# A hybrid encoder layer on one Trainium2 core: buffers of their own for some raw weight blocks and for G, low parts of the weights last, squares tied to later casts

## The chip, the cores and the metric

The kernel runs on 1 core of one Trainium2 chip. The metric is the device time in microseconds (us) of one execution of the whole program; lower is better. It is written in Bass with the Tile framework: tile pools hand out buffers, a scheduler orders the instructions of most engines, and semaphores carry the dependences. The engines in play are the TensorE (PE: matmuls, with its weight loads, PEld), the VectorE (DVE), the ScalarE (ACT), GpSimd (POOL) and the SyncE (SP), whose queue starts nearly all DMAs.

## The reference

One layer with sandwich norms around both sub-layers. Batch 1, S = 512 positions, D = 2048, FF = 4096 (twice that in the up projection), all float32.

```python
h = rms_norm(x, norm_gains[l, 0])
(sb_q, ..., sc_x) = jnp.split(h @ w_in[l], 11, axis=-1)      # 2048 x 5632
# four head groups: stick-breaking and differential attention, RG-LRU, short convolution
mixed = jnp.concatenate([y_sb, y_df, y_lru, y_sc], axis=-1) @ w_out[l]   # 2048 x 2048
x = x + rms_norm(mixed, norm_gains[l, 1])
h = rms_norm(x, norm_gains[l, 2])
u = causal_dwconv(h @ ffn_w_up[l], ffn_conv_w[l])            # 2048 x 8192, three taps
g, up = jnp.split(u, 2, axis=-1)
x = x + rms_norm((gelu(g) * up) @ ffn_w_down[l], norm_gains[l, 3])   # 4096 x 2048
```

## The kernel before

**Split numbers.** Activations lie transposed, as tiles of 128 channels by 512 positions. Each float32 operand is split into a high part, rounded to the matmul's type (float32r), and a low part, the rest. A product is three matmuls: high by high, high by low, low by high (`matmul3`, L120 to L125). Weights come from memory as raw blocks of 512 KB, 128 x 1024 numbers (`chunk`, L88 to L101, buffers `w_raw`); the ScalarE casts the high part (`w_hi`, L99), the VectorE subtracts to get the low part (`w_lo`, L100). Each of these three names has three buffers in the pool `wp`.

**Stages**, with their place in the profiled span:
- 0 to about 640 us: the in projection in `group`s, with the four head groups' work beside it.
- To about 775 us: the out projection (`out_group`); its last two groups of columns are done for each half of the positions apart (`HALVES`, 256 wide). `SumSq` (from L770) gathers the sum of squares for a norm: the ScalarE squares, GpSimd adds (L785), and a matmul with ones (L795) adds over the partitions, with the last `direct` squares given to that matmul apart. `residual` (L807) scales the result, has GpSimd's DMA accumulate it into x (L818), squares the sum on the ScalarE (L822), adds the squares (L824), stores the new x, called x1 (L826), and scales it by the gains (L829). `norm2` makes the normed h with its high and low parts.
- 775 to about 873 us: `up_plain`, units 0 to 3 of the up projection in ordinary groups. `low_parts` (L883) makes the last low parts of h out of the tiles gh and gl, which are then free.
- 873 to 1531 us: 28 calls of `up_unit` (L977), units 4 to 31. Each multiplies a 2 x 2 arrangement of weight blocks a11, a12, a21, a22 with h in seven products instead of eight (Strassen's scheme), of 24 matmuls 128 x 256 each. The operands of the products are a11, a12, s2, s1, s3, s4, a22 in this order, with s3 = a11 + a21, s1 = a21 + a22, s2 = a11 + s1, s4 = a12 + s2. s1 is made by a DMA of GpSimd that accumulates a22 from memory into a21's tile (L1017); the other sums are adds on the VectorE (L995). `operand` (L987 to L990) splits each into `w_hi` (ScalarE) and `w_lo` (VectorE). The products' results go from their accumulators to the tiles `ub` by copies on the ScalarE (L1026, L1036, L1041, L1053) and adds on the VectorE (L1032, L1045, L1049); then come the convolution (L928, L930), the gelu (L933), the gated product (L938), called g, and its store to memory (`g_d`, L939).
- 1540 to about 1896 us: g is loaded back (L1082) and split into high and low parts (L160, L161), and the down projection runs in groups over it. The last norm and x1 (loaded again, L1107) make the output (`finish`, L1108 to L1111).

**What sets the order.** PE issues in the order in which the program is written (`manual_schedule`). `tick()` counts blocks of matmuls, and `at(block, fn)` places work beside a given block. The other engines are ordered by the scheduler with priorities; work under `high_priority(offset=AHEAD)` goes ahead. Each engine, and SP's queue too, works its list in order: an instruction that waits holds all behind it.

**Buffers around the change.** In a unit, a11, a21 and a12 are in the three buffers of `w_raw`; s3 and a22 (loaded a second time, L1037) are in the halves of gh and gl (`spare`, two of each, which alternate from unit to unit). In the down projection the tiles f that hold loaded g and x1 come from the pool t3f with 5 buffers, opened where the pools of the up projection have been closed.

Of the kernel before, what the change touches and what calls it, by code (L numbers as in the profile page):

```python
# [16 lines left out]
P = 128  # L17
# [31 lines left out]
def trunk(ctx: ExitStack, tc: tile.TileContext, xT, params, consts, wgate, w_in, w_out, w_up0, w_up, w_dn, out):  # L49
# [30 lines left out]
    def gain(i, k):  # L80
        return pc("g", i * KT + k)
# [38 lines left out]
    def matmul3(ps, sh, sl, mh, ml, first, last, more=False):  # L120

        kw = {"skip_group_check": True} if more else {}
        T.matmul(ps, lhsT=sh, rhs=mh, start=first, stop=False, **kw)  # L123
        T.matmul(ps, lhsT=sh, rhs=ml, start=False, stop=False, **kw)  # L124
        T.matmul(ps, lhsT=sl, rhs=mh, start=False, stop=last, **kw)  # L125

    def group(chunks, hi, lo, order, evac, pool_tile=mm_tile, ts=ALL, before=None, tokens_out=False):
# [5 lines left out]
        for c in range(n):  # L133
# [3 lines left out]
            wh, wl = chunks[c]() if callable(chunks[c]) else chunk(chunks[c], 2 if fine else 1)  # L137
            for u, kk in ([(u, kk) for kk in range(2) for u in range(4)] if fine else
# [619 lines left out]
    with ExitStack() as ph:  # L758
        big = ph.enter_context(tc.tile_pool(name="bigf", bufs=4))
        ffp = ph.enter_context(tc.tile_pool(name="ffp", bufs=2))  # L760
        up_ph = ph.enter_context(ExitStack())
        ph2 = up_ph.enter_context(tc.tile_pool(name="ph2", bufs=1))
        t2p = up_ph.enter_context(tc.tile_pool(name="t2f", bufs=8))
# [45 lines left out]
        def residual(hf):  # L809
# [167 lines left out]
        def up_unit(unit):  # L977
            src = w_up[unit - 4]

            def raw(a, b):  # L980
                with tc.high_priority(offset=AHEAD):
                    t = wp.tile([P, 2, S], F32, name="w_raw")
                    nc.sync.dma_start(out=t, in_=src[a, b])
                return by4(t)
# [12 lines left out]
            def product(ps, ops, name, first):  # L997
                hi, lo = ops
                th, tl = tops[name]
                for k in range(8):  # L1000
# [227 lines left out]
```

## Time and profile before

| what | us |
|---|---|
| median of 3 runs (lowest, highest) | 1920.5 (1918.5, 1921.66) |
| the profiled execution | 1920.45 |
| its span, first to last instruction | 1918.7 |
| PE busy | 1803.0 |
| PE waiting for a low part in the units (L990) | 54.0 |
| mean granted clock of PE | 0.981 |

The prediction shows the page's lines. In them PE, PEld, DVE, ACT, POOL and SP are the engines; SPq and POOLq are the queues of DMAs of an engine. A row of the waits gives who waited for whom: us in total, times, and the longest. A row of the timeline gives the start, the duration, engine, line, operation, the tile written and those read, and in brackets how long the engine was idle before it and what ended this. A row of the windows gives a stretch, its length, the busy time of each engine with its number of instructions, the granted clock, the DMA share and GB/s. A row of DMA issues gives the number, the size, and the median time from issue to landing.

### The profile page before, as it was taken

How to read it: one execution, taken by the hardware profiler on the slowest of the kernel's cores; microseconds unless marked ns; L12 is line 12 of the kernel's file. 1: busy time of each engine (PE TensorE's matmuls, PEld its weight loads, DVE VectorE, ACT ScalarE, POOL GpSimd, SP SyncE). 2: the span in 40 equal slices, each digit the busy share in tenths (PEclk: the TensorE clock that was granted, in tenths of full speed). 3: DMA queues.
4: the chain of work that ended last, by engine and by line, in shares of the span. 5: the costliest groups of instructions: out<-in, count | busy, mean ns of one | idle time of the engine just before them, and what ended most of it. 6: DMA issues, size and time to landing. Idle time of an engine off the chain costs nothing. (4 is left out here: it accounts for less than half of the span.)

```text
span 1918.7 us, 27629 instructions
## 1 busy us (share of the span) xinstructions
PE 1803.0 (94%) x11176; PEld 1621.4 (85%) x11176; DVE 1145.5 (60%) x1574; ACT 869.5 (45%) x1301; POOL 110.9 (6%) x163
## 2 busy tenths in 40 slices
PE   8999999999999998898998998899999889999995
PEld 6778788888888898897988888888988878888895
DVE  7883675756574247598766666666666762222364
ACT  6442676743343347574444444444444552221342
POOL 0000111100000112100000000000000000010101
PEclk9999999999999999898999999999999999999998
DMA  7234222333325358755444444444444483333465
GB/s 242 86 102 132 76 72 83 110 116 90 98 88 197 102 181 235 216 178 153 123 122 123 133 121 122 121 123 126 128 126 128 119 285 99 99 97 94 125 200 182
DMA packets 84073, 256.91 MB, mean 134 GB/s; under 512 B 9029, under 2 KB 13381, under 8 KB 83945
## 3 DMA queue, kind: packets, MB, share of 16 engines
q1 hardware_dynamic: 78184, 235.23, 39.5%
q0 software_dynamic: 5184, 18.88, 5.1%
q8 instruction: 87, 1.43, 0.3%
q10 hardware_dynamic: 576, 1.05, 0.1%
q14 instruction: 42, 0.34, 0.1%
HBM read 230.99 MB, written 21.24 MB: 131 GB/s over the span
## 5 line engine op out<-in xcount | busy, mean ns | idle before, releaser
L124 PE MATMUL mm<-al,w_hi 128*128 128x256 f32 (+1 forms) x2048 | 674.4, 329 | 0.0
L125 PE MATMUL mm<-ah,w_lo 128*128 128x256 f32 (+1 forms) x1824 | 615.8, 338 | 54.9 <-DVE w_lo L990 53.4
L123 PE MATMUL mm<-ah,w_hi 128*128 128x256 f32 (+1 forms) x1824 | 618.2, 339 | 8.1 <-ACT w_hi L99 6.9
L100 DVE TENSOR_TENSOR w_lo<-w_raw,w_hi 128x1024 fp32r<-128x1024 f32 (+1 forms) x249 | 306.2, 1230 | 406.0 <-ACT w_hi L99 405.3
L99 ACT CAST w_hi<-w_raw 128x1024 fp32r<-128x1024 f32 (+1 forms) x249 | 260.6, 1047 | 449.5 <-PE mm L124 285.9
L125 PEld LDWEIGHTS mm<-ah,w_lo 128*128 128x128 f32 x1824 | 351.5, 193 | 98.3 <-DVE w_lo L990 62.3
L124 PEld LDWEIGHTS mm<-al,w_hi 128*128 128x128 f32 x2048 | 395.7, 193 | 31.5 <-issue 1.0
L123 PEld LDWEIGHTS mm<-ah,w_hi 128*128 128x128 f32 x1824 | 351.7, 193 | 41.1 <-ACT w_hi L99 7.3
L989 ACT CAST w_hi<-w_raw 128x1024 fp32r<-128x1024 f32 x140 | 145.9, 1042 | 222.8 <-PE mm L124 128.3
L990 DVE TENSOR_TENSOR w_lo<-w_raw,w_hi 128x1024 fp32r<-128x1024 f32 x140 | 170.6, 1219 | 2.6 <-ACT w_hi L989 2.6
L123 PE MATMUL mm<-big,w_hi 128*128 128x256 f32 (+1 forms) x544 | 161.6, 297 | 8.5 <-ACT big L160 8.5
L125 PE MATMUL mm<-big,w_lo 128*128 128x256 f32 (+1 forms) x544 | 163.1, 300 | 0.3
L124 PE MATMUL mm<-big,w_hi 128*128 128x256 f32 (+1 forms) x544 | 161.2, 296 | 0.0
L995 DVE TENSOR_TENSOR w_raw<-w_raw 128x1024 f32<-128x1024 f32 x56 | 68.4, 1222 | 138.6 <-DMA w_raw<-in_w_up_dram 138.6
L123 PE MATMUL pa<-ah,w_hi 128*128 128x256 f32 (+1 forms) x384 | 117.2, 305 | 3.3 <-ACT w_hi L99 3.3
L125 PE MATMUL pa<-ah,w_lo 128*128 128x256 f32 (+1 forms) x384 | 117.2, 305 | 2.2 <-DVE w_lo L100 2.2
L124 PE MATMUL pa<-al,w_hi 128*128 128x256 f32 (+1 forms) x384 | 116.6, 304 | 0.0
L123 PEld LDWEIGHTS mm<-big,w_hi 128*128 128x128 f32 x544 | 104.4, 192 | 11.4 <-ACT big L160 8.8
L125 PEld LDWEIGHTS mm<-big,w_lo 128*128 128x128 f32 x544 | 104.2, 192 | 6.7 <-DVE w_lo L990 4.2
L124 PEld LDWEIGHTS mm<-big,w_hi 128*128 128x128 f32 x544 | 104.4, 192 | 3.0 <-DVE big L161 0.4
L123 PE MATMUL mm<-gh,w_hi 128*128 128x256 f32 (+1 forms) x320 | 100.3, 314 | 1.9 <-ACT ub L1026 1.9
L125 PE MATMUL mm<-gh,w_lo 128*128 128x256 f32 (+1 forms) x320 | 98.2, 307 | 0.6 <-DVE w_lo L990 0.6
(266 smaller groups left out, 2659.4 us busy)
## 6 DMA issues: line engine op xcount, KB each, us to landing
w_raw<-in_w_up_dram SPq DMA_DIRECT2D x116, 512.0 KB, 4.2
w_raw<-in_w_in_dram SPq DMA_DIRECT2D x87, 512.0 KB, 3.6
w_raw<-in_w_dn_dram SPq DMA_DIRECT2D x80, 512.0 KB, 3.7
w_raw<-in_w_out_dram SPq DMA_DIRECT2D x48, 512.0 KB, 3.6
gl<-in_w_up_dram SPq DMA_DIRECT2D x28, 512.0 KB, 7.0
w_raw<-in_w_up_dram POOLq DMA_DIRECT2D x28, 512.0 KB, 8.0
g_d<-f SPq DMA_DIRECT2D x32, 256.0 KB, 4.3
f<-g_d SPq DMA_DIRECT2D x32, 256.0 KB, 4.1
```

Source lines behind the costliest of these rows:

```text
L99: w_split.append(A.copy(out=hi[:, sl], in_=raw[:, sl]))
L100: V.tensor_tensor(out=lo[:, sl], in0=raw[:, sl], in1=hi[:, sl].bitcast(F32), op=ALU.subtract)
L123: T.matmul(ps, lhsT=sh, rhs=mh, start=first, stop=False, **kw)
L124: T.matmul(ps, lhsT=sh, rhs=ml, start=False, stop=False, **kw)
L125: T.matmul(ps, lhsT=sl, rhs=mh, start=False, stop=last, **kw)
L989: w_split.append(A.copy(out=by4(hi), in_=v))
L990: V.tensor_tensor(out=by4(lo), in0=v, in1=by4(hi).bitcast(F32), op=ALU.subtract)
L995: V.tensor_tensor(out=out, in0=a, in1=b, op=ALU.add)
```

## The change

Three things change in the kernel, and some buffers move with them.

1. In `group`, each chunk but the last (and but a first one that comes in two pieces) now issues its sixteen matmuls with the weights' high part first and the eight with the low part after them; so does `product` in a unit.
2. a11 and a21 of a unit are loaded into the halves of gh and gl; s3, a12 and a22 go to the three buffers of `w_raw`. The tiles for loaded g, and half of those for x1, get a pool of their own (`ystage`, 3 buffers), open from the start of the phase; t2f has 6 buffers instead of 8, t3f 3 instead of 5. The last norm's `SumSq` have 3 square tiles, and the second one hands one square less to the matmul.
3. In `residual`, the squares of x1 and the scaling are issued block by block, each tied behind the most recent weight cast, and `norm2` comes 36 blocks later in both halves instead of 38 and 46.

```diff
     def group(chunks, hi, lo, order, evac, pool_tile=mm_tile, ts=ALL, before=None, tokens_out=False):
...
+            if not fine and c < n - 1:
+                for low in range(2):
+                    for u in range(4):
+                        us = slice(u * P, (u + 1) * P)
+                        for kk in range(2):
+                            k = order[2 * c + kk]
+                            if tokens_out:
+                                pairs = [(lo[k][:, us], wh[:, kk]), (hi[k][:, us], wh[:, kk])]
+                                pairs = [(hi[k][:, us], wl[:, kk])] if low else pairs
+                            else:
+                                pairs = [(wh[:, kk, us], hi[k][:, ts]), (wh[:, kk, us], lo[k][:, ts])]
+                                pairs = [(wl[:, kk, us], hi[k][:, ts])] if low else pairs
+                            for i, (a, b) in enumerate(pairs):
+                                T.matmul(pss[u], lhsT=a, rhs=b, start=c == 0 and kk == 0 and not low and i == 0,
+                                         stop=False)
+                        if u % 2 == 1:
+                            tick()
+                continue
...
+        ystage = ph.enter_context(tc.tile_pool(name="ystage", bufs=3))
...
-        t2p = up_ph.enter_context(tc.tile_pool(name="t2f", bufs=8))
+        t2p = up_ph.enter_context(tc.tile_pool(name="t2f", bufs=6))
...
                 G.dma_start(out=xs[q][:, hf], in_=mg[q][:, hf], accum_op=ALU.add)
-            for k in range(0, KT, 2):
-                x1 = xs[k // 4][:, hf, k % 4:k % 4 + 2]
-                sq = acc if k == 0 else ph2.tile([P, 2, S // 2], F32, name="q2", bufs=2)
-                A.activation(out=sq, in_=x1, func=AF.Square)
-                if k > 0:
-                    V.tensor_tensor(out=acc, in0=acc, in1=sq, op=ALU.add)
-                if k % 4 == 2:
-                    nc.sync.dma_start(out=x1_d[k // 4][:, hf], in_=xs[k // 4][:, hf])
-            for k in range(KT):
-                h = xs[k // 4][:, hf, k % 4]
-                A.activation(out=h, in_=h, func=AF.Copy, scale=gain(2, k))
-            at(clock[0] + (38, 46)[hf], lambda: norm2(hf, acc))
+                at(clock[0] + 18 + 3 * q, lambda q=q: squares(hf, q, acc))
+                at(clock[0] + 25 + 3 * q, lambda q=q: scale_h(hf, q))
+            at(clock[0] + 36, lambda: norm2(hf, acc))
+
+        def squares(hf, q, acc):
+            with tc.issue_after(w_split[-1].ins):
+                for i in range(2):
+                    n = 2 * q + i
+                    sq = acc if n == 0 else ph2.tile([P, 2, S // 2], F32, name="q2", bufs=2)
+                    A.activation(out=sq, in_=xs[q][:, hf, 2 * i:2 * i + 2], func=AF.Square)
+                    if n > 0:
+                        V.tensor_tensor(out=acc, in0=acc, in1=sq, op=ALU.add)
+            nc.sync.dma_start(out=x1_d[q][:, hf], in_=xs[q][:, hf])
...
             def product(ps, ops, name, first):
...
-                    ks = slice(k * P, (k + 1) * P)
-                    matmul3(ps, hi[:, ks], lo[:, ks], th[k], tl[k], first and k == 0, k == 7, not first)
+                    w = hi[:, k * P:(k + 1) * P]
+                    T.matmul(ps, lhsT=w, rhs=th[k], start=first and k == 0, stop=False, **kw)
+                    T.matmul(ps, lhsT=w, rhs=tl[k], start=False, stop=False, **kw)
                     if k % 2 == 1:
                         tick()
+                for k in range(8):
+                    T.matmul(ps, lhsT=lo[:, k * P:(k + 1) * P], rhs=th[k], start=False, stop=k == 7, **kw)
...
-            s3, a22 = spare[turn[0] % 2], spare[2 + turn[0] % 2]
+            n = turn[0] % 2
             turn[0] += 1
...
-            a11, a21 = raw(0, 0), raw(1, 0)
+            a11, a21 = raw(spare[n], 0, 0), raw(spare[2 + n], 1, 0)
+            s3, a12, a22 = (by4(wp.tile([P, 2, S], F32, name="w_raw")) for _ in range(3))
             add(s3, a11, a21)
...
-            a12 = raw(0, 1)
+            raw(a12, 0, 1)
...
-                nc.sync.dma_start(out=a22, in_=a22_src)
+            raw(a22, 1, 1)
...
-        t2p = ph.enter_context(tc.tile_pool(name="t3f", bufs=5))
+        t2p = ph.enter_context(tc.tile_pool(name="t3f", bufs=3))
...
-                y = t2()
                 with tc.high_priority(offset=AHEAD):
+                    y = ystage.tile([P, S], F32, name="ys")
                     nc.sync.dma_start(out=y, in_=g_d[4 * n + i])
...
-        ss3 = [SumSq("q3", 4), SumSq("q3", 4, 2)]
+        ss3 = [SumSq("q3", 3), SumSq("q3", 3)]
...
-                x1 = t2().rearrange("p (k t) -> p k t", k=2)
+                x1 = t2() if n % 2 == 0 else ystage.tile([P, S], F32, name="ys")
+                x1 = x1.rearrange("p (k t) -> p k t", k=2)
```

The scheduler moves more than the diff shows. First the VectorE in the middle of the units, from the low part of s1 of one unit to s2 of the next; in the rows of before L990 makes a low part, L995 is an add of blocks, L1032 and L1045 add a product to `ub`, L938 is the gated product.

```order
L990 TENSOR_TENSOR w_lo<-w_raw,w_hi 128x1024
L938 TENSOR_TENSOR f_9032<-f_9032,f_9002 128x512
L1032 TENSOR_TENSOR ub<-ub,mm 128x256
L915 MEMSET ub 128x2
L990 TENSOR_TENSOR w_lo<-gh,w_hi 128x1024
L995 TENSOR_TENSOR gh<-w_raw 128x1024
L990 TENSOR_TENSOR w_lo<-w_raw,w_hi 128x1024
L990 TENSOR_TENSOR w_lo<-gl,w_hi 128x1024
L1045 TENSOR_TENSOR ub<-ub,mm 128x256
L990 TENSOR_TENSOR w_lo<-w_raw,w_hi 128x1024
L995 TENSOR_TENSOR w_raw<-w_raw 128x1024
```

Of the change, the same place (L1014 for L990, L1019 for L995, L963 for L938, L1061 for L1032, L1074 for L1045):

```order
L1014 TENSOR_TENSOR w_lo<-gl,w_hi 128x1024
L955 SCALAR_TENSOR_TENSOR f_9035<-ub,neg_w,f_9035 128x512
L963 TENSOR_TENSOR f_9035<-f_9035,f_9005 128x512
L940 MEMSET ub 128x2
L1061 TENSOR_TENSOR ub<-ub,mm 128x256
L1014 TENSOR_TENSOR w_lo<-w_raw,w_hi 128x1024
L1019 TENSOR_TENSOR w_raw<-gh,gl 128x1024
L1014 TENSOR_TENSOR w_lo<-w_raw,w_hi 128x1024 x2
L1074 TENSOR_TENSOR ub<-ub,mm 128x256
L1014 TENSOR_TENSOR w_lo<-gh,w_hi 128x1024
L1019 TENSOR_TENSOR gh<-gh,gl 128x1024
```

The order of the VectorE stays the same but for one convolution step; what moved is where the operands lie: s3 is read from gh and gl and written to `w_raw`, and s2 is made within gh.

Second, SP's queue over one unit, between two stores of g. In before:

```order
L939 DMA g_d_112<-f_7872 128x512
L983 DMA w_raw<-in_w_up_dram 128x1024
L1037 DMA gl<-in_w_up_dram 128x1024
L983 DMA w_raw<-in_w_up_dram 128x1024 x2
L939 DMA g_d_113<-f_8104 128x512
```

Here the first row is the load of a12, the second that of a22, and the x2 are a11 and a21 of the next unit. In the change:

```order
L1007 DMA w_raw<-in_w_up_dram 128x1024 x2
L964 DMA g_d_112<-f_7875 128x512
L1007 DMA gh<-in_w_up_dram 128x1024
L1007 DMA gl<-in_w_up_dram 128x1024
L964 DMA g_d_113<-f_8107 128x512
```

Now the x2 are a12 and a22 of one unit, and the loads into gh and gl are a11 and a21, for a unit that comes two turns after the one whose buffers they take.

Third, the ScalarE between two copies of the products' results. In before (L1053 copies the last product, L928 and L933 are a convolution's first tap and the gelu, L1026 copies the next unit's first product):

```order
L1053 COPY ub<-mm 128x256
L928 ACTIVATE f_10424<-ub,neg_w 128x512
L989 CAST w_hi<-w_raw 128x1024
L1026 COPY ub<-mm 128x256
L933 ACTIVATE f_10394<-f_10394 128x512
L989 CAST w_hi<-gh 128x1024
```

Of the change (L1082, L953, L958 and L1055 are the same four):

```order
L1082 COPY ub<-mm 128x256
L953 ACTIVATE f_10427<-ub,neg_w 128x512
L1013 CAST w_hi<-gl 128x1024
L958 ACTIVATE f_10397<-f_10397 128x512
L1055 COPY ub<-mm 128x256
L1013 CAST w_hi<-w_raw 128x1024 x2
```

The copy of the first product moved from ahead of the gelu to behind it.

More of the change, by code (lines that the diff above doesn't have):

```diff
@@ L118, in flush, with matmul3 @@
             tick()
[L120 to L125, printed above, removed]
+    def matmul3(ps, sh, sl, mh, ml, first, last):
+        T.matmul(ps, lhsT=sh, rhs=mh, start=first, stop=False)
+        T.matmul(ps, lhsT=sh, rhs=ml, start=False, stop=False)
+        T.matmul(ps, lhsT=sl, rhs=mh, start=False, stop=last)
     def group(chunks, hi, lo, order, evac, pool_tile=mm_tile, ts=ALL, before=None, tokens_out=False):
@@ L818, in residual, with scale_h @@
                 G.dma_start(out=xs[q][:, hf], in_=mg[q][:, hf], accum_op=ALU.add)
[L819 to L830 removed]
+                at(clock[0] + 18 + 3 * q, lambda q=q: squares(hf, q, acc))
[10 more added lines that the diff above has]
+            nc.sync.dma_start(out=x1_d[q][:, hf], in_=xs[q][:, hf])
+        def scale_h(hf, q):
+            with tc.issue_after(w_split[-1].ins):
+                for i in range(4):
+                    h = xs[q][:, hf, i]
+                    A.activation(out=h, in_=h, func=AF.Copy, scale=gain(2, 4 * q + i))
         def norm2(hf, acc):
@@ L978, in up_unit, with raw @@
             src = w_up[unit - 4]
-            def raw(a, b):
+            def raw(t, a, b):
                 with tc.high_priority(offset=AHEAD):
-                    t = wp.tile([P, 2, S], F32, name="w_raw")
-                    nc.sync.dma_start(out=t, in_=src[a, b])
-                return by4(t)
+                    nc.sync.dma_start(out=t, in_=by4(src[a, b]))
+                return t
             def operand(v):
```

1 line of the change is left out of this document (added).

## The prediction

> **What bounds the kernel now.** I read the page first (busy time, then the slices), then the waits of the TensorE, then one unit's rows on every engine, because an average over stages does not say which wait ends last.
>
> ```profile
> span 1918.7 us, 27629 instructions
> PE 1803.0 (94%) x11176; PEld 1621.4 (85%) x11176; DVE 1145.5 (60%) x1574; ACT 869.5 (45%) x1301; POOL 110.9 (6%) x163
> PE   8999999999999998898998998899999889999995
> ```
>
> PE is the bound nearly everywhere: 94% busy, and what is not PE is 116 us in all. The slices with an 8 are the middle of the program, the 28 split units (about 870 to 1531 us), and the places where a stage hands over. So the change can only win in these places; in the long projections PE has no idle time to give back. The waits of PE say what the missing time waits for (total, times, longest):
>
> ```profile
> PE mm L125 <- DVE w_lo L990: 54.0, 45, 2.4
> PE mm L123 <- ACT big L160: 8.5, 1, 8.5
> PE mm L123 <- DVE ub L1045: 5.1, 1, 5.1
> PE pa L795 <- POOL ss L785: 4.6, 2, 4.3
> ...
> PE pa L125 <- DVE w_lo L100: 2.2, 4, 0.8
> PE mm L125 <- DVE w_lo L100: 1.5, 2, 0.8
> ...
> PE mm L123 <- ACT ub L1041: 1.3, 1, 1.3
> ```
>
> One wait is 54 of them: a unit's products wait for a low part from the VectorE. Next, the same stretch by windows, from the second product of the eighth unit (unit 7) to that of the last; it is 24 units long (4032 matmuls at 168 each), and the second window is ahead of the down projection:
>
> ```profile
> core 0: us, PE busy (x) PEld busy (x) DVE busy (x) ACT busy (x) POOL busy (x), PEclk, DMA share, GB/s
> 951.75:1514.08 562.33, 510.51 (x4032) 496.56 (x4032) 381.30 (x477) 244.49 (x337) 20.90 (x24) 0.98 0.45 123
> 1536.80:1543.70 6.90, 3.35 (x7) 2.43 (x8) 3.22 (x5) 3.08 (x6) 0.00 (x0) 0.51 0.84 271
> 1600.00:1700.00 100.00, 100.00 (x443) 82.81 (x442) 22.26 (x18) 23.79 (x31) 4.59 (x6) 1.00 0.33 100
> ```
>
> A unit takes 562.33 / 24 = **23.43 us**. Its matmuls start 0.12 us apart when nothing holds them:
>
> ```profile
> 1111.80 0.28 PE L125 MATMUL mm<-ah,w_lo 128*128 128x256 f32 x1
> 1111.92 0.28 PE L123 MATMUL mm<-ah,w_hi 128*128 128x256 f32 x1
> ```
>
> so PE needs 168 x 0.12 = **20.16 us** of it, and 3.27 us are lost per unit. No engine is full (DVE 381 of 562), so it is a loop of dependences. Here it is on the VectorE in one unit, in order:
>
> ```profile
> 1103.17 1.23 DVE L995 TENSOR_TENSOR gh<-w_raw 128x1024 f32<-128x1024 f32 x1 [2.25 <-DMA w_raw<-in_w_up_dram]
> 1104.32 1.22 DVE L990 TENSOR_TENSOR w_lo<-w_raw,w_hi 128x1024 fp32r<-128x1024 f32 x1
> ...
> 1113.96 1.23 DVE L995 TENSOR_TENSOR w_raw<-w_raw 128x1024 f32<-128x1024 f32 x1 [5.82 <-DMA w_raw<-in_w_up_dram]
> ...
> 1115.43 1.22 DVE L990 TENSOR_TENSOR w_lo<-w_raw,w_hi 128x1024 fp32r<-128x1024 f32 x1
> ...
> 1123.69 1.22 DVE L990 TENSOR_TENSOR w_lo<-gh,w_hi 128x1024 fp32r<-128x1024 f32 x1
> ...
> 1127.24 1.23 DVE L995 TENSOR_TENSOR gh<-w_raw 128x1024 f32<-128x1024 f32 x1 [2.34 <-DMA w_raw<-in_w_up_dram]
> ```
>
> s3 = a11+a21 (1103.17) must be done before GpSimd may start the DMA that accumulates a22 into a21; s2 = a11+s1 (1113.96) waits for that DMA; 10.9 us of VectorE work follow, and the next s3 (1127.24) then waits for the next a21 to be loaded. Behind s2 stands the low part of a12 (1115.43), for which PE waits:
>
> ```profile
> 1116.70 0.38 PE L125 MATMUL mm<-ah,w_lo 128*128 128x256 f32 x1 [2.23 <-DVE w_lo L990]
> ```
>
> The loop's two waits, summed over the 28 units:
>
> ```profile
> DVE w_raw L995 <- DMA w_raw<-in_w_up_dram: 138.6, 28, 6.0
> DVE gh L995 <- DMA w_raw<-in_w_up_dram: 60.3, 28, 2.6
> ```
>
> So the loop is: 10.9 work, 60.3/28 = **2.15 waiting for a21**, 1.2 for s3, and some 9.2 from the end of s3 to s2 (23.43 less the others), nearly all of it the accumulating DMA:
>
> ```profile
> w_raw<-in_w_up_dram POOLq DMA_DIRECT2D x28, 512.0 KB, 8.0
> DMA to landing us min/median/max: 6.3/8.0/9.0
> ```
>
> **The change, part by part.** The profiled execution took 1920.45 us, 1.75 more than its span, and the median of the runs shown is 1920.5; I sum against the span and add 1.75.
>
> *Own buffers for a11 and a21.* Their buffers were those of the last raw blocks, so their loads were issued when the low parts of the unit before were done; SP waited 545 us for that in total (`SPq L983 <- DVE w_lo L990`):
>
> ```profile
> SPq L983 <- DVE w_lo L990: 545.2, 80, 13.5
> ```
>
> Now two pairs alternate, and each load is issued more than a unit ahead of its use, 20 us where a load of a raw block takes 4.2 (quoted below). The 2.15 us wait goes. What is late next is the accumulating DMA, which stays in the loop: 23.43 - 2.15 = **21.28 us**, still over PE's 20.16. 24 units x 2.15 = **-51.7 us**. s3, a12 and a22 now share the raw buffers in a fixed order; a12 is loaded when the low part of s4 of the unit before is done (the row at 1104.32, 2.4 us after s3 starts) and is wanted some 8 us later, behind s2, so its load is covered by the accumulating DMA, beside which it runs, as two plain loads do already. Were that cover gone, each us would cost 24.
>
> *Low parts last.* A product now does its 16 matmuls with the high part first, so its low part may come 16 x 0.12 = 1.92 us later. It takes the 2.2 us stall in the second product nearly away, but by itself it moves only the place of the wait: a loop of 21.28 makes PE wait 1.1 us per unit somewhere, I think at the third product, whose accumulator must first be copied out by the ScalarE; that copy now stands behind the gelu. So no term of its own in the units. In the output projection's halves the six waits for w_lo L100 (2.2 + 1.5 = 3.7, longest 0.8) are all shorter than 1.92 and vanish: **-3.4**, leaving 0.3 for the one or two instructions in their place. In the stretches where PE is 100.00 busy the new order gains nothing. Its price: the four accumulators are visited twice per chunk. In the 100 us window quoted above PE has no idle time with a change of accumulator at every sixth matmul, so I take 0; the upper end is rival D.
>
> *First units.* The first s3 of before:
>
> ```profile
> 869.11 1.23 DVE L995 TENSOR_TENSOR gh<-w_raw 128x1024 f32<-128x1024 f32 x1 [1.33 <-DMA w_raw<-in_w_up_dram]
> ```
>
> gh and gl are free only when the low parts of h are made, so the first s3 comes an estimated 1 to 3 us later than before, and the queue also carries three early loads of g, each behind its own store. But the waits for the copies L1045 and L1041 (5.1 + 1.3) fall away, because that add no longer stands behind an s2 that waits: -6.4 + 2.9 = **-3.5**, bounds +3 and -9.
>
> *Squares.* Before and after, they stand at nearly the same casts on the ScalarE; norm2 of the second half is 10 blocks earlier, and PE does not wait for it there. 0; bounds +2 and -4.6 (the whole wait for `ss`).
>
> *Up to down.* PE waits 8.5 us for the first g, whose load needed a buffer of the old phase:
>
> ```profile
> 1540.35 0.79 PE L123 MATMUL mm<-big,w_hi 128*128 128x512 f32 x1 [8.55 <-ACT big L160]
> f<-g_d SPq DMA_DIRECT2D x32, 256.0 KB, 4.1
> ```
>
> With buffers of their own, three loads and casts are done long before; I leave 0.5: **-8.0**. The window quoted above shows the clock at 0.51 just after the gap, with 3.35 us of matmuls in it; half of that goes too: **-1.7**.
>
> *Tail.* The last x1 waits for a free buffer, the store before it having to land:
>
> ```profile
> 1914.66 0.69 DVE L1110 TENSOR_TENSOR f<-m,f 128x512 f32<-128x512 f32 x1 [4.64 <-DMA out_dram<-f]
> 1911.41 0.32 SPq L1107 DMA_DIRECT2D f<-x_d  x1
> ```
>
> Six buffers for five: the 4.6 goes, less about 1 because GpSimd's last adds and their stores end then, and because the sum of squares keeps one add more on GpSimd ahead of its matmul: **-3.5** (bounds 0, -4.6).
>
> Sum: 51.7 + 3.4 + 3.5 + 8.0 + 1.7 + 3.5 = 71.8. Span 1918.7 - 71.8 = 1846.9, and 1.75 on it: **1848.7 us**.
>
> **Rivals.**
>
> *A. PE bounds the units.* If the accumulating DMA lands in its shortest 6.3 rather than 8.0, the loop is 19.6, below PE's 20.16; a unit then takes about 20.3, 24 x 3.13 = 75.1 instead of 51.7, sum 95.2: **1825 us**. For it: its source is now a block with no second reader close by. Against it: two plain loads of 512 KB still run beside it. The Trainium skill ("DMA: Bandwidth & Descriptors", "Anatomy of one DMA — SWDGE (gpsimd) path") fits a GpSimd DMA as about 2.0 us plus bytes over 436 GB/s, which for 512 KB is an estimate of 3.2 us; by that the loop would be far below PE and this rival certain. The trace's 8.0, never under 6.3, does not agree for a DMA that accumulates, so the rival keeps only the chance that those two numbers give it.
>
> *B. The accumulating DMA gets slower,* since prefetched loads and the g store now fall beside it. The same kind of DMA took 10.3 where two were in flight:
>
> ```profile
> gl<-big POOLq DMA_DIRECT2D x4, 512.0 KB, 10.3
> w_raw<-in_w_up_dram SPq DMA_DIRECT2D x116, 512.0 KB, 4.2
> ```
>
> 8.0 to 9.2, half of the way, makes the loop 22.5: 24 x 1.2 = 28.8 back, **1877 us**. At 10.3 the loop is 23.6 and nothing is left of the units' gain: 1900.
>
> *C. The change doesn't do what it says:* SP works in order, and a wait ahead of the a21 load (for a raw buffer or a store) may hold it as long as before. Then only 20.1 is won: **1900 us**.
>
> *D. Slower.* The new order changes the accumulator after 4 and then after 2 matmuls instead of 6. Should PE idle a little at each change, the clock may drop. The group stages are about 100 to 870 and 1540 to 1900, 1,100 us of PE; the clock window quoted shows 0.51 as the low state, so each us at it loses half. From 144 us in that state (13% of the stages) the gain of 71.8 is gone; at 20% the time is 1848.7 + 110 = **1959 us**. Against it: in the 100 us window that already has a change at each sixth matmul PE is 100.00 busy at 1.00. The Trainium skill ("TensorE: Matmul & The Clock Gate", "A second HAM failure mode: psum-queue depth-cycling") says just this, that cycling through accumulator banks lets the clock oscillate; by it the old order would show it too, and the trace does not agree there.
>
> **How the numbers follow.** Forecast 1848.7 with its own range 1840 to 1858: 0.60. A 0.17, B 0.15 (the part under 1880 included in the range), C 0.05, D 0.03. The range runs from A with a full win in the first units (1820) to B (1880) and leaves out C, D and the worst of B. About 0.2% (4 us) is what a measurement of this kernel can tell from no change. Faster 0.95 (all but D and a little), same 0.02 (B at its worst with losses in the first units), slower 0.03.
>
> **What would show it.** Right: the wait of s3 for the a21 load near zero, s2 still waiting for the accumulating DMA in each unit, 24 units in about 511 us, some 1 us of wait per unit at the third product and hardly any for a low part; no wait of 8 us ahead of the down projection; no store waited for in the tail. Wrong: a unit of 20.3 with s2 no longer waiting (A); a median of the accumulating DMA over 9 (B); s3 waiting as before (C); a clock under 1.00 in the window of 100 us (D).

## The result: 1919.5 to 1816.0 us, further than forecast

The changed kernel takes **1815.95 us** (median of 4 runs, 1814.78 to 1817.2) against 1919.53 for the kernel before beside it: a ratio of 0.9459, 95% interval 0.9443 to 0.9476. The forecast was 1848.7 with a range down to 1820, so the direction was right and the forecast gain of 71.8 too small by some 32. The page of the changed kernel, with the rows that answer to those of before:

```profile
span 1815.5 us, 27679 instructions
PE 1768.2 (97%) x11174; PEld 1602.3 (88%) x11174; DVE 1156.8 (64%) x1574; ACT 874.1 (48%) x1301; POOL 109.4 (6%) x164
PE   8999999999999999899899999999999999999995
```

The 8s of the middle are gone: from the fourth split unit on, no slice of PE is under 90% until the last norm. The waits of PE (total, times, longest) show the same. The first row of before, 54.0 us for a low part in the units, has shrunk to one wait in the first unit, and the 8.5 us ahead of the down projection is gone:

```profile
PE pa L813 <- POOL ss L803: 5.9, 2, 4.8
PE mm L121 <- ACT w_hi L99: 5.5, 1, 5.5
PE pa L150 <- ACT w_hi L99: 4.3, 3, 2.0
PE mm L1032 <- DVE w_lo L1014: 2.7, 1, 2.7
...
PE mm L1027 <- ACT ub L1055: 0.6, 2, 0.3
```

The windows show where some 103 us of the span went. First the stretch from the first unit to the third product of the fourth, in before and then in the changed kernel, and then the 24 units from that product to the same product of the last unit:

```profile
872.70:954.50 81.80, 71.06 (x554) 69.79 (x552) 60.53 (x83) 37.67 (x55) 2.61 (x3) 0.94 0.46 122
```

```profile
869.00:942.70 73.70, 68.78 (x554) 67.67 (x553) 62.58 (x86) 38.60 (x56) 3.49 (x4) 0.98 0.56 162
942.75:1426.59 483.84, 483.84 (x4034) 483.84 (x4033) 394.03 (x477) 250.09 (x337) 20.89 (x24) 1.00 0.49 142
```

483.84 / 24 = **20.16 us a unit, which is PE's own time to the hundredth**, where the forecast had a loop of 21.28. PE is busy 483.84 of 483.84 us at a clock of 1.00.

The same places in both traces (the start of the matmul with the same number), term by term:

| stretch of PE | before, us | after, us | saved | forecast |
|---|---|---|---|---|
| start to the first unit | 872.7 | 869.0 | 3.7 | 3.4 |
| first unit to the third product of the fourth | 81.8 | 73.7 | 8.1 | 3.5 |
| 24 units | 562.3 | 483.8 | **78.5** | **51.7** |
| third product of the last unit to the down projection | 23.5 | 14.4 | 9.1 | 8.0 |
| down projection to the last matmul | 357.6 | 356.2 | 1.5 | 1.7 |
| last matmul to the end | 20.8 | 18.3 | 2.4 | 3.5 |
| sum | | | 103.3 | 71.8 |

Of the 31.5 us that the forecast lacked, 26.8 are in the 24 units and 4.6 in the first ones. So the question is what became of the accumulating DMA, which was to hold each unit at 21.28. On the VectorE, in one unit of the changed kernel (s3, the next low part, s2, the low part of a12, and the s3 of the next unit):

```profile
1105.89 1.23 DVE L1019 TENSOR_TENSOR w_raw<-gh,gl 128x1024 f32<-128x1024 f32 x1
1107.24 1.23 DVE L1014 TENSOR_TENSOR w_lo<-w_raw,w_hi 128x1024 fp32r<-128x1024 f32 x1
...
1114.53 1.23 DVE L1019 TENSOR_TENSOR gh<-gh,gl 128x1024 f32<-128x1024 f32 x1
...
1116.41 1.23 DVE L1014 TENSOR_TENSOR w_lo<-w_raw,w_hi 128x1024 fp32r<-128x1024 f32 x1 [0.24 <-ACT w_hi L1013]
...
1126.06 1.23 DVE L1019 TENSOR_TENSOR w_raw<-gh,gl 128x1024 f32<-128x1024 f32 x1
```

s3 no longer waits for its load (no bracket), as forecast. But neither does s2 wait for the accumulating DMA: it follows s3's end by 7.4 us instead of the forecast's 9.2, and the DMA has by then been done for 1.3 us (median of the 24 units). That wait, 138.6 us over 28 units in before, is now 8.9 us in 5 units. The row of the VectorE's waits:

```profile
DVE gh L1019 <- DMA gl<-in_w_up_dram: 8.9, 5, 3.6
```

The reason stands in the rows of DMA issues: the DMA itself takes 5.8 us instead of 8.0 (median from issue to landing), and never more than 7.0.

```profile
gl<-in_w_up_dram POOLq DMA_DIRECT2D x28, 512.0 KB, 5.8
```

```profile
DMA to landing us min/median/max: 5.2/5.8/7.0
```

In the units just behind the first ones, where the operands still catch up with PE, the loop runs at 19.4 to 19.9 us (periods of s2: 19.91, 19.37, 19.50, 19.66). That is about what the loop takes by itself, and it is below 20.16. So the explanation sought is of 2.2 us in one DMA.

### The profile page after: what moved, and what is told of

It is laid out like the page before. It is cut to its first block, busy times and chain, and to the rows that moved or that the text cites. A ratio compares the mean times of both kernels' runs of the same rounds, so it can differ in the third digit from the quotient of the medians.

```text
span 1815.5 us, 27679 instructions
## 1 busy us (share of the span) xinstructions
PE 1768.2 (97%) x11174; PEld 1602.3 (88%) x11174; DVE 1156.8 (64%) x1574; ACT 874.1 (48%) x1301; POOL 109.4 (6%) x164
## 4 chain that ended last, share of the span: by engine, by line
PE 84%; DVE 5%; issue 4%; ACT 3%; DMA 3%; POOL 0%; SPq 0%; POOLq 0%; DVEq 0%; ACTq 0%
PE mm L150 38%; PE mm L1027 10%; PE mm L1028 10%; PE mm L1032 10%; PE pa L150 8%; PE mm L121 2%; PE mm L123 2%; PE mm L122 1%; DVE w_lo L100 1%; PE pa L578 1%; DMA x_d<-gh 1%; ACT w_hi L99 1%; DMA gh<-big 1%; PE pa L683 1%; DVE vd L270 0%
## 5 line engine op out<-in xcount | busy, mean ns | idle before, releaser
L150 PE MATMUL mm<-ah,w_hi 128*128 128x512 f32 (+1 forms) x1000 | 353.4, 364 | 2.8 <-DVE t L321 2.1
L150 PE MATMUL mm<-al,w_hi 128*128 128x512 f32 (+1 forms) x1000 | 351.2, 361 | 0.0
L150 PE MATMUL mm<-ah,w_lo 128*128 128x512 f32 (+1 forms) x1000 | 226.7, 365 | 0.0
L1028 PE MATMUL mm<-al,w_hi 128*128 128x256 f32 x896 | 219.8, 283 | 0.0
L150 PEld LDWEIGHTS mm<-ah,w_lo 128*128 128x128 f32 x1000 | 169.8, 190 | 27.6 <-issue 1.5
L1014 DVE TENSOR_TENSOR w_lo<-w_raw,w_hi 128x1024 fp32r<-128x1024 f32 x112 | 136.9, 1223 | 46.5 <-ACT w_hi L1013 44.1
L1027 PE MATMUL mm<-ah,w_hi 128*128 128x256 f32 x672 | 165.0, 283 | 1.1 <-ACT w_hi L1013 1.1
L1027 PE MATMUL mm<-big,w_hi 128*128 128x256 f32 x448 | 110.0, 283 | 0.5 <-ACT ub L1065 0.5
L1028 PE MATMUL mm<-big,w_hi 128*128 128x256 f32 x448 | 109.9, 283 | 0.0
L1032 PE MATMUL mm<-ah,w_lo 128*128 128x256 f32 x672 | 94.7, 284 | 2.7 <-DVE w_lo L1014 2.7
L1032 PEld LDWEIGHTS mm<-ah,w_lo 128*128 128x128 f32 x672 | 86.9, 192 | 2.9 <-DVE w_lo L1014 2.9
L1013 ACT CAST w_hi<-gh 128x1024 fp32r<-128x1024 f32 x56 | 58.7, 1048 | 60.7 <-PE mm L1028 55.1
L1027 PEld LDWEIGHTS mm<-big,w_hi 128*128 128x128 f32 x448 | 86.0, 192 | 0.7 <-ACT ub L1065 0.7
```

What stands on the lines that cost most here:

```text
L150: T.matmul(pss[u], lhsT=a, rhs=b, start=c == 0 and kk == 0 and not low and i == 0, stop=False)
L1013: w_split.append(A.copy(out=by4(hi), in_=v))
L1014: V.tensor_tensor(out=by4(lo), in0=v, in1=by4(hi).bitcast(F32), op=ALU.subtract)
L1027: T.matmul(ps, lhsT=w, rhs=th[k], start=first and k == 0, stop=False, **kw)
L1028: T.matmul(ps, lhsT=w, rhs=tl[k], start=False, stop=False, **kw)
L1032: T.matmul(ps, lhsT=lo[:, k * P:(k + 1) * P], rhs=th[k], start=False, stop=k == 7, **kw)
```

## The experiments

Two theories of it stood at the start: **contention** (fewer bytes beside it) and **buffer** (it accumulates into another tile, or one loaded long before). A third, a **race**, came up only with the packet records (below). Each run is one edit of the kernel before or of the changed one.

**1. The second load of a22 out of the way (kernel before).**

```diff
             add(a11, a11, s1)
             s2 = a11
+            with tc.high_priority(offset=AHEAD):
+                V.tensor_copy(out=a22[:, 0, 0:2], in_=s2[:, 0, 0:2])
```

> The kernel before, with one edit: the second load of a22 may start only when s2 is made, so that it no longer runs beside the DMA that accumulates a22 into a21. Theory of contention (the accumulating DMA takes 8.0 us in the kernel before because two plain loads of 512 KB are in flight beside it, and 5.8 us in the changed kernel because only one is for most of its time): its median falls to about 6 (5.2 to 6.6), a unit from 23.43 to about 21.4 us, the time from 1919.5 to about 1870 (1862 to 1882). Rival theory (the buffer into which it accumulates, or that a21 had just landed in it, sets its time): the median stays at 8.0, a unit at 23.4, the time at 1915 to 1922.

Measured: 1903.5 us, ratio 0.9922 (0.9904 to 0.9939). The row of the DMA:

```profile
w_raw<-in_w_up_dram POOLq DMA_DIRECT2D x28, 512.0 KB, 7.3
```

8.0 fell to 7.3 only, and a unit from 23.43 to 548.2/24 = 22.84. So the second load beside the DMA costs 0.7 us in the kernel before, not the 2.2 looked for, and the time of 1903.5 lies between the two ranges that were expected.

**2. One more transfer beside it (changed kernel).**

```diff
                 G.dma_start(out=a21, in_=a22_src, accum_op=ALU.add)
+                nc.sync.dma_start(out=side, in_=s3)
```

`side` is a tile in memory that nothing reads.

> The changed kernel, with one more transfer of 512 KB per unit beside the accumulating DMA (a store of s3 to memory that nothing reads). Contention: the accumulating DMA goes from 5.8 to about 8 us, the loop from the 19.4 that the catching-up units 3 to 5 of the changed kernel show to 21.3 to 21.6, above PE's 20.16, so the time goes from 1816 to about 1847 (1838 to 1855). Rival (the buffer sets it): 5.8, a unit of 20.16, 1815 to 1819.

Measured: 1837.0 us, ratio 0.9578 (0.9555 to 0.9601), a unit 499.9/24 = 20.83. The row of the DMA:

```profile
gl<-in_w_up_dram POOLq DMA_DIRECT2D x28, 512.0 KB, 8.0
```

The kernel is again bound by the loop as soon as the DMA is back at 8.0, in the direction of contention, a little under the range expected. By the packet records (below) the first packet of the DMA comes only 0.4 us later than in the changed kernel, and the other 1.8 us are in its transfer: this added store, issued 0.38 us ahead of GpSimd's DMA, costs more than the load of run 1. This run also has what the forecast assumed, own buffers and a DMA of 8.0, and even so its unit is 20.83 and not 21.28.

**3. One pair of buffers (changed kernel).**

```diff
-            n = turn[0] % 2
+            n = 0
```

> The changed kernel with one pair of buffers for a11 and a21 instead of two that alternate, so that each load is issued as late as in the kernel before. Contention theory: the accumulating DMA stays near 5.8, s3 waits about 2.2 us per unit for a21, the loop is 19.4 + 2.2 = 21.6 and the time about 1850 (1842 to 1858): the early loads and the shorter DMA are worth about the same, and each alone leaves the loop above PE's 20.16. Rival (that a21 had just landed in the buffer sets the DMA's time): 8.0 us again, a unit of 23.5 to 23.8, about 1898. If the early loads are worth nothing: 1816.

Measured: 1822.5 us, ratio 0.9497 (0.948 to 0.9515), by the row of the DMA 6.4:

```profile
gl<-in_w_up_dram POOLq DMA_DIRECT2D x28, 512.0 KB, 6.4
```

None of the three expected times came: the early load, the change's stated device, is worth only 6.5 us when the DMA is short. And here the two plain loads follow the accumulating DMA by 0.76 and 1.89 us, nearly as in the kernel before (0.52 and 1.65), yet it takes 6.4 and not 8.0. Loads that follow this closely are so not enough to make it 8.0, and neither is it that a21 has only just landed.

**The race.** The packet records of GpSimd's queue show more. In one unit of the kernel before GpSimd issues the accumulating DMA and SP the load of a12 so (rows of the timeline, start and duration first):

```profile
1105.04 0.89 POOL L1017 DMA_DIRECT2D w_raw<-in_w_up_dram  x1 [22.17 <-DVE gh L995]
```

```profile
1105.56 0.33 SPq L983 DMA_DIRECT2D w_raw<-in_w_up_dram  x1
```

and in the changed kernel:

```profile
1107.53 0.86 POOL L1046 DMA_DIRECT2D gl<-in_w_up_dram  x1 [19.29 <-DVE w_raw L1019]
```

```profile
1108.49 3.20 SPq L1007 DMA_DIRECT2D w_raw<-in_w_up_dram  x2
```

SP follows by 0.52 us in the one and by 0.97 in the other. The packets of these two units, counted from GpSimd's issue: in before the first packet of a12 starts at 1.47 us and that of the accumulating DMA only at 3.65; in the changed kernel the accumulating DMA's first starts at 1.56, and a12's at 4.56. In both, the second starts 2 to 3 us behind the first.

The margin is small. After the end of s3, GpSimd issues its DMA 0.64 us later in the kernel before and 0.41 us later in the changed kernel, and SP the load of a12 1.16 us later in the one and 1.16 to 1.38 in the other (all 24 units). GpSimd's quarter of a microsecond alone makes 0.52 to 0.76. The first packet of a12 comes 0.96 us after SP's issue in before, that of the accumulating DMA 1.58 us after GpSimd's in the changed kernel (medians); from these two an estimate is that the order turns where SP follows by 0.62. Nothing in the change aims at this, and why GpSimd issues sooner the runs don't show: that the order turned was luck.

The 24 steady units of each of ten kernels (both kernels, runs 1 and 3, and some below), sorted by when the SP queue issued its load relative to GpSimd:

```
SP's load, us after GpSimd's issue   units   first packet, us (10%..90%)   DMA, us   kernels
-0.65 to -0.43 (ahead)                  44   2.2  (2.0..2.5)               7.9       runs 6, 12
 0.23 to  0.53 (just behind)            72   3.6  (3.4..3.7)               8.0       before, runs 1, 7
 0.69 to  1.26                         100   1.6  (1.6..1.6)               5.7       changed, runs 3, 4, 6, 8
 1.66 to  2.07                          24   1.6  (1.6..1.7)               5.4       run 5
```

No unit falls between 0.53 and 0.69, and the estimated 0.62 lies in this gap. It is still only a correlation; run 5 turns the order by itself.

**5. The load of a12 later (kernel before).**

```diff
-            a12 = raw(0, 1)
+            with tc.high_priority(offset=AHEAD):
+                a12 = by4(wp.tile([P, 2, S], F32, name="w_raw"))
+                if turn[1:]:
+                    V.tensor_copy(out=a12[:, 0, 0:2], in_=turn.pop()[:, 0:2].bitcast(F32))
+                nc.sync.dma_start(out=a12, in_=by4(src[0, 1]))
...
+            turn.append(o22[1])
             product(x, o22, "T4", False)
```

> The kernel before, with the load of a12 tied behind the last low part of the unit before (a copy of two columns), so that it is issued some 1.8 us after GpSimd's accumulating DMA instead of 0.52. Theory of the race: in the kernel before the a12 load reaches the DMA engines first, and the accumulating DMA's first packet comes 3.6 us after its issue, against 1.6 in the changed kernel, where a12 is issued 0.97 us after it. With the race turned, its first packet comes at 1.6 us, its median falls from 8.0 to about 6 (5.4 to 6.7), a unit from 23.4 to about 21.4 us, the time from 1919 to about 1872 (1860 to 1885). Rival (only the bytes in flight beside it matter): the median stays at 7.3 to 8.0, the time at 1903 to 1920.

Measured: 1882.4 us, ratio 0.9807 (0.9794 to 0.9821).

```profile
w_raw<-in_w_up_dram POOLq DMA_DIRECT2D x28, 512.0 KB, 5.4
```

First packet at 1.6 us, the DMA at 5.4, with the tiles, the buffers and the bytes of the kernel before. So the time of the DMA is turned by the moment of one load, and the buffer theory falls. Run 1 is the counterpart: there the load of a22 was moved, a12's stayed at 0.52, and the first packet stayed at 3.6. The VectorE's work beside GpSimd's issue is not the cause either: in the unit of before shown above and one of this run (from 1089.61 us) a low part starts 0.41 us behind the issue in both, another at 1.87 and 2.08, and GpSimd's row of the issue is 0.89 us long in both. The time came out 10 us above the expectation: s2 followed s3's end by 6.1 us instead of 8.8 (medians), but the scheduler put two convolution steps ahead of low parts, and the way from s2 to the next s3 grew from 13.2 to 14.5 us. A unit is 528.3/24 = 22.0.

**6 and 12. GpSimd later (changed kernel).** A small GpSimd operation ahead of the accumulating DMA, on 256 columns in the first run and on 2 in the second:

```diff
+                G.tensor_scalar(out=a21[:, 0], in0=a21[:, 0], scalar1=1.0, scalar2=0.0, op0=ALU.mult, op1=ALU.add)
                 G.dma_start(out=a21, in_=a22_src, accum_op=ALU.add)
```

> The changed kernel, with a small GpSimd operation (a quarter of a21 times 1.0) ahead of the accumulating DMA, so that this is issued 0.5 to 0.9 us later and no more than 0.5 us ahead of the a12 load. Race: its first packet comes at about 3.6 us, its median goes from 5.8 to about 7.5 to 8, the loop to 19.4 + 0.7 + 2 = 22.1, and 24 units cost 1.9 each: 1816 + 46 = about 1862 (1850 to 1875). Rival (the race doesn't matter): the loop is 19.4 + 0.7 = 20.1, still under PE's 20.16, and the time stays at 1816 to 1820.

> As the run with the small GpSimd operation, but on two columns, so that the accumulating DMA is issued some 0.5 us later and a12's load some 0.5 us behind it, as in the kernel before. This is what the prediction assumed: own buffers, and the accumulating DMA as long as before. Race: the first packet at 3.6 us, median 7.5 to 8, loop 11.1 + 1.2 + 9.6 = 21.9, 1816 + 42 = 1858 (1848 to 1862). Rival (no race): loop 19.9, 1816 to 1818. If the operation takes so long that a12's load goes 0.6 us ahead, as in most units of that other run: first packet at 2.0, 1850 to 1858.

Measured: 1855.3 us, ratio 0.9665 (0.9649 to 0.9681), and 1854.5, ratio 0.9675 (0.9649 to 0.9701). GpSimd's rows of the second, and then its row of DMA issues:

```profile
1128.25 1.09 POOL L1046 TENSOR_SCALAR gl<-gl 128x2 f32<-128x2 f32 x1 [20.96 <-DVE w_raw L1019]
1129.74 0.89 POOL L1048 DMA_DIRECT2D gl<-in_w_up_dram  x1 [0.41 <-POOL gl L1046]
```

```profile
gl<-in_w_up_dram POOLq DMA_DIRECT2D x28, 512.0 KB, 7.8
```

The operation took 1.09 us even on two columns, so SP's load went 0.43 us ahead, and the case "just behind" could not be made this way: the first packet came at 2.3 us. But a load ahead costs as much, 7.8 us in all, most of it in the transfer. The unit is 525.5/24 = 21.9 us. The 1855 is near the 1848.7 of the forecast, but it does not bear the forecast out: the added operation is in the loop too. From the end of s3 to the issue it is 1.6 us here and 0.4 in the changed kernel, and without these 1.2 us a unit would be an estimated 20.7, as the 20.83 of run 2. **With the change in place and the DMA at 8.0, run 2's 1837 is the better measure.** So the two runs show that the longer DMA binds the loop again; the case of 3.6 us to the first packet was made only in the kernel before.

**4. The old order of the matmuls (changed kernel).** `group` and `product` as in the kernel before.

> The changed kernel with the old order of the matmuls (high, high, low for each weight tile) in all chunks and products. My theory: in the units the loop of 19.4 us is shorter than PE's work, so PE falls behind the operands and the order is worth nothing there; it is worth the 3.7 us before the first unit and up to 2 us in the first units: 1816 + 4 to 6 = 1820 to 1822. Rival (low parts last is what lets PE run without gaps): PE waits for a low part in each unit, units of 21 us and more, 1836 or more.

Measured: 1817.2 us, ratio 0.9476 (0.9458 to 0.9495), not to be told from the changed kernel and below the range expected. A unit is 20.16 with either order, as soon as PE is the bound.

**7. The new order of the matmuls alone (kernel before).**

> The kernel before with the new order of the matmuls alone (low parts last in chunks and products). My theory: the loop through the accumulating DMA sets a unit's 23.4 us, so only the place of PE's wait moves, and outside the units it is worth 0 to 4 us: 1914 to 1920. Rival (the stalls for low parts are what costs): the 54 us of PE's waits for L990 go, 1870.

Measured: **1888.7 us, ratio 0.9842 (0.9828 to 0.9857)**: 31 us, where I had expected 0 to 4. The accumulating DMA is still at 8.0 and its first packet at 3.6, but s3's wait for a21 fell from 60.3 us:

```profile
DVE gh L1012 <- DMA w_raw<-in_w_up_dram: 26.5, 26, 2.2
```

PE's waits for a low part of a unit, 54.0 us in before, are gone from its rows; in their place it waits for the ScalarE's copy of a product:

```profile
PE mm L1020 <- ACT ub L1047: 37.4, 16, 4.4
```

So PE's wait did move, as the theory had it, but the loop also became shorter, and the trace puts that on the VectorE. In this kernel the low part of s1 (the row at 1110.17, s2 having started at 1103.29) stands ahead of the last convolution step, not behind it:

```profile
1110.17 1.22 DVE L1007 TENSOR_TENSOR w_lo<-w_raw,w_hi 128x1024 fp32r<-128x1024 f32 x1
...
1111.30 0.75 DVE L947 SCALAR_TENSOR_TENSOR f<-ub,neg_w,f 128x512 f32<-128x512 f32 x1
...
1115.16 1.23 DVE L1012 TENSOR_TENSOR gh<-w_raw 128x1024 f32<-128x1024 f32 x1 [0.84 <-DMA w_raw<-in_w_up_dram]
```

It ends 8.1 us after s2's start instead of 8.9, the buffer of a21 is free so much earlier, and the load comes that much sooner. From s2 to the next s3 it is some 11.9 us instead of 13.2, and a unit 535.8/24 = 22.3. I put the gain down to the order in which the scheduler then put the VectorE, and not to the order of the matmuls itself. (That this reordering is all of the 1.1 us a unit was read from the trace and not tried by itself.)

**10. The squares as before (changed kernel).**

> The changed kernel with the squares, scaling and norm2 of x1 as in the kernel before. My step: worth nothing, 1814 to 1818. Rival: the squares tied to casts shortened the stretch before the first unit, 3 to 5 us more, 1819 to 1821.

Measured: 1824.6 us, ratio 0.9516 (0.9503 to 0.9529): the new squares are worth some 9 us, more than either expectation had. The matmul of norm2's second half starts at 810.0 instead of 803.1, and the first units then are, by windows,

```profile
867.50:946.40 78.90, 70.88 (x554) 70.27 (x553) 66.27 (x90) 40.23 (x57) 3.50 (x4) 0.94 0.53 155
```

78.9 us at a clock of 0.94, against 73.7 at 0.98 in the changed kernel. PE waits there for a copy by the ScalarE, where the changed kernel has no such wait over 0.5 us:

```profile
PE mm L1020 <- ACT ub L1063: 4.1, 1, 4.1
```

The first unit starts 1.5 us earlier here, so 3.7 us are left between these two traces, whose executions took 1821.2 and 1817.2 us; the medians of the timed runs are 8.6 apart.

**11. The staging pool as before (changed kernel).**

> The changed kernel without the pool for g and x1 (pools t2f and t3f, and the last sums of squares, as in the kernel before). My steps: the wait ahead of the down projection comes back (9.1 us between the two kernels at this place), half clock behind it (1.5) and the end (2.4): 1816 + 13 = 1829 (1826 to 1832). Rival (the units' shorter loop ends early enough that g is loaded in time anyway): 1816 to 1820.

Measured: 1829.7 us, ratio 0.9538 (0.9525 to 0.9551), as expected. The wait is back:

```profile
PE mm L150 <- ACT big L177: 7.8, 1, 7.8
```

**8 and 9. Further on.** What PE still waits for outside the ends: GpSimd's adds of squares ahead of the first unit, and the low part of a12 behind s2 in the first unit.

```diff
-        ss1 = [SumSq("q1", 4), SumSq("q1", 4)]
+        ss1 = [SumSq("q1", 4), SumSq("q1", 4, 4)]
```

> The changed kernel, with the last four squares of the second half's out projection given to the matmul with ones, instead of GpSimd adding three of them (3 adds took 5.93 us there, with PE waiting 4.8 us for them and at half clock behind it). If GpSimd's adds end that wait: 1816 less 3 to 5, 1811 to 1813. If the ScalarE's squares end it: 1815 to 1817.

and with it, for the first unit:

```diff
             o11 = operand(a11)
-            add(a11, a11, s1)
+            o12 = operand(a12) if unit == 4 else None
+            with tc.issue_after(lows[-1].ins):
+                add(a11, a11, s1)
             s2 = a11
-            o12 = operand(a12)
+            o12 = o12 or operand(a12)
```

(`lows` holds the instructions that make low parts.)

> The changed kernel with the four squares given to the matmul, as in the run before, and in the first unit the low part of a12 tied ahead of s2 on the VectorE. In the changed kernel s2 waits there 3.58 us for the accumulating DMA with that low part behind it, PE waits 2.97 us for the low part, and a stretch of 3.4 us at half clock follows. If that is all: 1814 less 3 to 4.5, 1809.5 to 1811. If PE then only waits for s2 itself at the third product: 1813 to 1815.

Measured: 1814.0 us, ratio 0.9447 (0.9435 to 0.946); with the second edit too, 1812.4, ratio 0.9452 (0.944 to 0.9465). Both waits are gone from the rows, but the intervals overlap that of the changed kernel (0.9443 to 0.9476): whether these are faster than it can't be said, and neither time is in a range that was expected.

## Why the prediction was wrong

- **The step that failed** is "What is late next is the accumulating DMA, which stays in the loop: 23.43 - 2.15 = 21.28 us". The DMA does stay in the loop, but the term of 9.2 us for it was carried over from the old trace as if it were its own price. Of the 2.2 us between 8.0 and 5.8, some 2 were the a12 load, issued half a microsecond behind it and first to move data (3.6 against 1.6 us to the first packet); the rest is in the transfer. The change moves the loads beside it: in the unit shown SP's load starts 0.97 and not 0.52 us behind GpSimd's, and the second one 3.84 and not 1.66. With the DMA at 5.8 the loop is under PE's 20.16 (19.4 to 19.9 where it shows by itself), PE is the bound, and 24 x 1.12 = 26.9 us more are won. The sum was too high by another 0.45 us a unit: with the DMA at 8.0 in the changed kernel (run 2) the loop is 20.83.
- "beside which it runs, as two plain loads do already": this sentence held the error. It treated the loads beside the DMA as cover for them and not as part of its price; the second load was far behind it in the changed kernel, which SP's rows of the order could not show, since they have no times.
- **Rival A was what happened**, with the mechanism that it named (a shorter accumulating DMA, PE as the bound) and 0.17 for a chance. Its unit of 20.3 was 20.16, and its 1825 lacked the 4.6 of the first units and 3.4 of the units. Its reason "against" (two plain loads still run beside it) was the wrong one. Its reason "for" (no second reader of the block close by) is worth 0.7 us at most, by run 1, which moved that second load away; so the mechanism that made the DMA short, the order of two loads, was not in the forecast, and the rival came true in part by luck. The fit of the Trainium skill ("DMA: Bandwidth & Descriptors", "Anatomy of one DMA — SWDGE (gpsimd) path"), an estimate of 3.2 us for 512 KB, spoke for this rival; the shortest such DMA in any run took 5.0 (run 10), so the runs don't agree with it for a DMA that accumulates, beside other loads, though the rival came true.
- **Early loads: the wait went, but the term of 2.15 us is not theirs alone, and not additive.** s3's wait for a21 is gone, as forecast. But run 3 shows that without them only 6.5 us are lost, because the loop then is 20.3 and PE's floor takes the rest. From s2 to the next s3 it is 13.2 us in before, 11.9 with the new order of the matmuls alone (run 7), 12.0 in the changed kernel with one pair of buffers (run 3), and 11.1 with two where the loop binds (run 2): of these 2.1 us, the second pair gives 0.9.
- **Low parts last: right in the change, wrong alone.** It was given no term in the units, and in the changed kernel it has none (run 4). Alone it gives 31 us, as far as the trace shows through the VectorE's order; the section on the change shows that one convolution step moves there, and the prediction did not price it. The 3.4 before the first unit was booked to it; the total there was 3.7, but run 4 keeps all but 0.9 of that, so most of it has another source.
- **Squares: "0" was wrong.** They are worth some 9 us (run 10), nearly twice the bound of 4.6 given on that side. In the traces 3.7 of it stand in the first units, whose gain was forecast 4.6 too small (3.5, measured 8.1): with norm2 earlier, they run without run 10's wait of 4.1 us for a copy, and at a clock of 0.98 instead of 0.94. How the earlier norm2 ends that wait was not followed further.
- **Up to down, half clock, tail:** 9.1, 1.5 and 2.4 against 8.0, 1.7 and 3.5, and run 11 gave 13.7 for the three (13.2 forecast). Right.
- **B, C and D:** the DMA got faster, not slower; s3 doesn't wait; so C did not happen either. In the down projection, whose groups now change the accumulator after 4 and after 2 matmuls, PE is busy all the time at a clock of 1.00, so D did not happen:

```profile
1434.00:1776.00 342.00, 342.00 (x1825) 296.96 (x1824) 128.09 (x134) 118.32 (x157) 18.75 (x25) 1.00 0.48 151
```

A unit of 21.6 to 21.9 us, on the way to B's 22.5, came only where an added operation held up GpSimd (runs 6 and 12).

The parts do not add up: the loop before is 23.43, PE's floor 20.16, and the shorter DMA, the early load and, as far as the trace shows, the VectorE's order each remove a part of the 3.27 between them. All together go below the floor, so that taking one away costs little: a unit is 20.3 without the early load (run 3) and 20.8 with the DMA back at 8.0 (run 2).

## What to carry to other kernels

When a DMA is in the loop, read not only its time to landing but when its first packet starts and what the other queues issue within a microsecond of it; its time in the old trace is not its price once the loads around it move. Compute the engine's own floor (matmuls times their spacing) first and price a shortened loop as reaching that floor at most, with its chance weighed by how near the loop is. A reordered instruction on an engine that is not the bound can still free a buffer earlier; where the order shows such a move, price it.

## What the runs showed of the hardware

- The accumulating DMA of 512 KB that GpSimd issues starts its first packet 1.6 us after its issue, or at 3.6 if SP's load of 512 KB is issued 0.23 to 0.53 us behind it; at 0.69 us and more it keeps its 1.6. A load issued 0.4 to 0.65 us ahead of it costs less at the start (2.2) but more in the transfer (7.9 us in all). All three are in the table above. Why a load that is first by a tenth of a microsecond costs more at the start than one that is half a microsecond ahead, the records don't say.
- A GpSimd operation on 128 x 2 numbers took 1.09 us in this loop (run 12).
- PE ran 24 units, 484 us, without any idle time in the record and at a clock of 1.00, and 342 us of the down projection as well, where it changes the accumulator after 4 and after 2 matmuls.
